# The projections' product P2 nested for pairs of rope units, and the plan's table of shifted due times left out

## Chip, cores and metric

The kernel runs on one core of one Trainium2 chip. The metric is the device time of one execution in microseconds, the median of several runs. TensorE does the matrix products, VectorE and ScalarE the elementwise work, GpSimd a little of it, and SyncE (SP) starts the transfers.

## What is computed

Two sequences of 512 tokens and width 1024 (`x_prompt`, `x_sample`) go through the same trunk of two layers.

```
x = x + diff_attention(rms_norm(x))      # layer 1: w_in 1024 x 8192 -> q, k, v, gate; w_out 2048 x 1024
x = x + bidir_retention(rms_norm(x))     # layer 2: w_in 1024 x 6144 -> q, k, v, gate; w_out 2048 x 1024
y = rms_norm(x)
```

q and k are rotated (`rotary_half`, `retention_rotate`), the gate goes through SiLU and multiplies the mixer's output ahead of `w_out`. Everything is float32. The change is in the first product of each layer, `h @ w_in`.

## The kernel before

**Three passes.** Every operand of a product is split into a high part `hi` (a rounding to fp32r, written by ScalarE, helper `hi_of`, L450) and a low part `lo = x - hi` (VectorE, `lo_of`, L453). A product is the three passes hi*hi, hi*lo, lo*hi (`PASSES`), each with its own load of the 128 x 128 stationary operand.

**Seven products.** Both sequences stand side by side: the activations B are 1024 x 1024 (width x tokens of both). They are cut into 2 x 2 blocks, B11 and B21 for the first sequence (upper and lower half of the width), B12 and B22 for the second. `make_b` builds from them the seven operands B11, B21, T1, T2, B22, T3, T4, four row tiles of 128 x 512 each, split in hi and lo and kept in slots (`B_OF`, `B_SLOT`). A `Unit` is 256 columns of `w_in`: its weights are 2 x 2 blocks of 512 x 128. It takes seven products instead of eight, in the order `SEQ`: P1 = A11*B11, P2 = A12*B21, P5, P6, P3, P7, P4. The products P5, P6, P3 and P7 have weights that are sums of blocks (`combine` in `Unit.prep`, L620, on VectorE); P1, P2 and P4 take blocks as they were loaded. A product of a "pair" unit (rope or gate) is 4 row tiles x 3 passes = 12 matmuls of 128 x 512 (L671, `Unit.product`). A "wide" unit (the values v) has 512 columns and its matmuls are 128 x 256 (L681), 48 to a product. `Unit.evac` adds the products up: ScalarE copies P1, P5 and P6's bank (L724), VectorE adds the copies to P2, P3 and P7's banks (L732).

**Units.** Layer 1 has 16 rope units (q and k of 8 heads), 8 gates and 4 wides, layer 2 has 8, 8 and 4. The first five units of a layer are gates, whose products are interleaved so that they need the operands in the order in which `make_b` has them. Behind these `mixed` puts two rope units, then a wide or a gate, and so on; layer 1 ends on six rope units and two gates. `rot_done` rotates: 4 multiplications, 2 sums and 2 splits on VectorE for each sequence of a unit, then stores. `gate_done` (L826 to L829) and `v_done` finish the others.

**Order.** `projections` walks the list of `product_order` and prepares the weights (sum, hi, lo) in a ring `ws` of `WS_BUFS` = 7 places ahead of the product that uses them. Every operation of the kernel is recorded in a `Plan` with an engine, a cost, what it reads and what it writes. `Plan.arrange` then simulates the engines and writes the order of each engine: TensorE takes products in the program's order, or passes over those that aren't ready within a window of 24; the others take what is ready by due time. `Plan.issue` repeats that for eight rounds, feeds the begins back as due times and keeps the best. On top of it lies a table `SHIFTS` of 45 entries (place in time, stretch behind it, size, share, seed). Each moves the due times of some operations near its place by random amounts, and the order is arranged again after each.

**Buffers.** `raw` (4 tiles of loaded weights), `st` (3 weight sums of 1024 columns), `c` (4 copies), `e` (8 sums), `m` (4), `os` (3 outgoing). PSUM has eight banks: pj 3, sc 2, o 2, tp 1. A rope unit in the middle of a layer uses pj for P1, P6, P7 and P4, sc for P5 and P3, o for P2 alone.

Of the kernel before, what the change touches and what calls it, by code (L numbers as in the profile page):

```python
# [16 lines left out]
P = 128  # L17
# [16 lines left out]
WS_BUFS = 7  # L34
LAG = 4
# [12 lines left out]
class Buf:  # L48
# [19 lines left out]


SHIFTS = (  # L70
# [14 lines left out]
)  # L85


class Plan:
# [167 lines left out]
    def issue(self, rounds=8):  # L256
# [29 lines left out]
def trunk_kernel(  # L286
# [14 lines left out]
    wk = ctx.enter_context(tc.tile_pool(name="wk", bufs=1))  # L301
    pj = ctx.enter_context(tc.tile_pool(name="pj", bufs=1, space=bass.MemoryType.PSUM))
# [4 lines left out]
    SIZE = dict(raw=1024, st=1024, c=512, e=512, m=512, os=1024)  # L307
# [3 lines left out]
    def view(pool, tag, i, size, shape, dt=F32):  # L311
# [3 lines left out]
        if (tag, i) not in places:  # L315
            if size <= 32 and pool in (cp, wk):
                k = next(k for k, used in enumerate(gaps) if used + size <= PAD - 32)
# [13 lines left out]
    def work(tag, shape, bufs, dt=F32, name=None):  # L331
        size = SIZE.get(tag, shape[1])
# [3 lines left out]
    gaps = [0] * (WS_BUFS - 1)  # L336
    arena = ar.tile([P, 18 * 1024 + 128], F32R, tag="arena", name="arena")
    rings, pads = [], []
    for i in range(WS_BUFS):
        rings.append(ar.tile([P, 1024 + 32], F32R, tag=f"ws{i}", name=f"ws_{i}"))  # L340
        if i < WS_BUFS - 1:
            pads.append(ar.tile([P, PAD - 32], F32, tag=f"pad{i}", name=f"pad_{i}"))

    def slot(n, shape, dt=F32R, shift=0):
# [5 lines left out]
        if at is None:  # L350
# [3 lines left out]
            return Buf(plan, f"b{n}", 1, lambda i: cp.tile(shape, dt, tag=f"b{n}", name=label))  # L354
# [13 lines left out]
    def ws_t(shape, wide=False):  # L368
# [1327 lines left out]
```

## Time and profile before

| what | value |
|---|---|
| median of 3 runs | 1790.91 us (1790.78 to 1790.96) |
| span of the profiled execution, first to last instruction | 1789.1 us |
| TensorE busy | 1780.3 us |
| VectorE busy | 1483.1 us |
| ScalarE busy | 894.0 us |
| GpSimd busy | 117.3 us |
| granted TensorE clock | 1.000 |

The profiled execution is one run with a span of 1789.1 us; the median of the timed runs is 1.8 us above that. In the profile, PE is TensorE's matmuls, PEld its weight loads (beside the matmuls), DVE VectorE, ACT ScalarE, POOL GpSimd, and SPq the transfers that SyncE issues. A group reads: line, engine, operation, names out<-in, shapes, count, then busy time, mean ns of one, and the idle time ahead of it with what ended it. In a row of windows each engine has its busy us and, in brackets, its number of instructions. A matmul's end is modelled and overlaps the next one's start, so a busy TensorE isn't yet TensorE at its pace; the distance from start to start tells that. By the stretches of the trace, the five gates and the building of B take up to some 107 us, layer 1's projections run to about 630 us, attention to about 1020, layer 2's projections to about 1490 and retention to the end.

### The profile page before, as it was taken

How to read it: one execution, taken by the hardware profiler on the slowest of the kernel's cores; microseconds unless marked ns; L12 is line 12 of the kernel's file. 1: busy time of each engine (PE TensorE's matmuls, PEld its weight loads, DVE VectorE, ACT ScalarE, POOL GpSimd, SP SyncE). 2: the span in 40 equal slices, each digit the busy share in tenths (PEclk: the TensorE clock that was granted, in tenths of full speed). 3: DMA queues.
4: the chain of work that ended last, by engine and by line, in shares of the span. 5: the costliest groups of instructions: out<-in, count | busy, mean ns of one | idle time of the engine just before them, and what ended most of it. 6: DMA issues, size and time to landing. Idle time of an engine off the chain costs nothing.

```text
span 1789.1 us, 27780 instructions
## 1 busy us (share of the span) xinstructions
PE 1780.3 (100%) x10317; PEld 1564.5 (87%) x10317; DVE 1483.1 (83%) x2401; ACT 894.0 (50%) x1866; POOL 117.3 (7%) x256
## 2 busy tenths in 40 slices
PE   9999999999999999999999999999999999999998
PEld 7889889898988888888888888898989988888887
DVE  8968788778698888888888897877887968888887
ACT  8754344343444555455445876444434455444446
POOL 1000000000000011111111100000000000111114
PEclk9999999999999999999999999999999999999999
DMA  6444554655545695455453524464646559664652
GB/s 220 138 139 142 169 164 145 192 162 153 186 118 179 205 334 205 175 188 189 170 189 124 188 75 139 149 205 165 222 135 232 166 196 395 251 228 177 235 212 95
DMA packets 162815, 328.81 MB, mean 184 GB/s; under 512 B 12772, under 2 KB 76920, under 8 KB 162680
## 3 DMA queue, kind: packets, MB, share of 16 engines
q1 hardware_dynamic: 162352, 326.71, 53.8%
q8 instruction: 81, 1.33, 0.3%
q14 instruction: 54, 0.44, 0.1%
q10 hardware_dynamic: 328, 0.34, 0.1%
HBM read 209.55 MB, written 117.44 MB: 183 GB/s over the span
## 4 chain that ended last, share of the span: by engine, by line
PE 99%; DMA 0%; ACT 0%; DVE 0%; issue 0%; POOLq 0%; SPq 0%; DVEq 0%; ACTq 0%
PE pj L671 22%; PE pj L984 20%; PE sc L671 11%; PE pj L681 10%; PE o L671 9%; PE o L1312 5%; PE sc L1251 5%; PE sc L681 5%; PE o L1521 2%; PE o L681 2%; PE sc L1477 1%; PE tp L1501 1%; PE o L1529 1%; PE pj L1292 1%; PE tp L1292 1%; PE tp L908 0%
## 5 line engine op out<-in xcount | busy, mean ns | idle before, releaser
L984 PE MATMUL pj<-ws,arena 128*128 128x512 f32 x1542 | 377.6, 392 | 0.0
L984 PEld LDWEIGHTS pj<-ws,arena 128*128 128x128 f32 x1542 | 281.8, 188 | 54.3
L671 PE MATMUL pj<-b,ws 128*128 128x512 f32 x1080 | 263.4, 390 | 0.0
L671 PEld LDWEIGHTS pj<-b,ws 128*128 128x128 f32 x1080 | 201.1, 188 | 41.0
L989 DVE SCALAR_TENSOR_TENSOR b<-pj,pad,b 128x512 f32<-128x512 f32 (+1 forms) x257 | 190.7, 745 | 24.1 <-PE pj L984 21.1
L453 DVE TENSOR_TENSOR ws<-raw,ws 128x512 fp32r<-128x512 f32 (+2 forms) x165 | 141.8, 864 | 66.6 <-ACT ws L450 56.3
L453 DVE TENSOR_TENSOR ws<-st,ws 128x512 fp32r<-128x512 f32 (+1 forms) x192 | 147.5, 774 | 55.6 <-ACT ws L450 49.5
L450 ACT CAST ws<-st 128x512 fp32r<-128x512 f32 (+1 forms) x192 | 131.9, 692 | 121.8 <-PE pj L671 42.6
L671 PE MATMUL sc<-arena,ws 128*128 128x512 f32 x768 | 185.1, 389 | 0.0
L671 PE MATMUL o<-arena,ws 128*128 128x512 f32 x744 | 178.5, 391 | 0.0
L450 ACT CAST ws<-raw 128x512 fp32r<-128x512 f32 (+2 forms) x165 | 126.1, 769 | 88.6 <-PE o L671 48.3
L671 PEld LDWEIGHTS sc<-arena,ws 128*128 128x128 f32 x768 | 144.0, 188 | 29.7
L671 PEld LDWEIGHTS o<-arena,ws 128*128 128x128 f32 x744 | 138.4, 188 | 28.5 <-DVE arena L513 0.2
L671 PE MATMUL pj<-arena,ws 128*128 128x512 f32 x636 | 156.0, 390 | 0.0
L671 PEld LDWEIGHTS pj<-arena,ws 128*128 128x128 f32 x636 | 118.6, 188 | 24.3
L1269 ACT ACTIVATE b<-sc,pad 128x512 f32<-128x512 f32 x128 | 87.6, 692 | 74.1 <-DVE pad L1259 74.0
L724 ACT COPY c<-pj 128x512 f32<-128x512 f32 x104 | 60.8, 586 | 117.8 <-PE pj L671 67.7
L681 PE MATMUL pj<-ws,b 128*128 128x256 f32 x960 | 116.9, 275 | 0.0
L681 PEld LDWEIGHTS pj<-ws,b 128*128 128x128 f32 x960 | 113.3, 188 | 0.6
L1251 PE MATMUL sc<-arena 128*128 128x512 f32 x384 | 101.3, 397 | 0.0
L1312 PEld LDWEIGHTS o<-arena 128*128 128x128 f32 x768 | 93.0, 188 | 2.5
L1312 PE MATMUL o<-arena 128*128 128x256 f32 x768 | 93.6, 277 | 0.0
(229 smaller groups left out, 2827.4 us busy)
## 6 DMA issues: line engine op xcount, KB each, us to landing
qk<-os SPq DMA_DIRECT2D x192, 256.0 KB, 3.5
arena<-qk SPq DMA_DIRECT2D x96, 512.0 KB, 6.6
v<-os SPq DMA_DIRECT2D x64, 512.0 KB, 5.2
arena<-v SPq DMA_DIRECT2D x64, 512.0 KB, 4.1
raw<-in_da_w_in_dram SPq DMA_DIRECT2D x63, 512.0 KB, 5.1
raw<-in_ret_w_in_dram SPq DMA_DIRECT2D x48, 512.0 KB, 4.9
os<-g SPq DMA_DIRECT2D x32, 512.0 KB, 7.9
g<-e SPq DMA_DIRECT2D x48, 256.0 KB, 4.7
```

The lines of the kernel that those rows point to most:

```text
L450: act(n, lambda: nc.scalar.copy(dst(), src()), r, w)
L453: dve(n, lambda: nc.vector.tensor_tensor(dst(), src(), hi().bitcast(F32), op=ALU.subtract), r, w)
L671: nc.tensor.matmul(ps.t, a[u][0]()[:, k, :], bt[k][:, v, :], start=(opens and k == 0 and i == 0), stop=(k == 3 and i == 2), skip_group_che ...
L681: nc.tensor.matmul(ps[:, (t % 2) * 256:(t % 2) * 256 + 256], bt[k][:, v, t * P:(t + 1) * P], a[u][0]()[:, k, :], start=(opens and t % 2 == ...
L724: act(S, lambda c=c, ps=ps: nc.scalar.copy(c.t, ps.t), [ps], [c])
L984: nc.tensor.matmul(ps[:, here], o[a][:, e, t * P:(t + 1) * P], u[b][:, e, here], start=(m == 0), stop=(m == 5))
L989: axpy(n, lambda half=half, here=here, ps=ps: nc.vector.scalar_tensor_tensor(half, ps[:, here], rr[:, t % 2:t % 2 + 1], half, op0=ALU.mult ...
L1251: nc.tensor.matmul(s.t, q[:, a, t * P:(t + 1) * P], k[:, b, :], start=(n == 0), stop=(n == 2))
L1269: act(840, lambda j=j, s=s, m=m: nc.scalar.activation(p[:, j, :], s.t, AF.Exp, bias=m.t, accum_out=sm[:, 2 * j + n:2 * j + n + 1]), [s, m] ...
L1292: nc.tensor.transpose(tp[:, j * P:(j + 1) * P], p[:, 0, j * P:(j + 1) * P], ident.t)
L1312: nc.tensor.matmul(o[:, e * 256:(e + 1) * 256], v[b][:, j, e * P:(e + 1) * P], aT[a][:, j, :], start=(n == 0), stop=(n % 12 == 11), skip_g ...
L1521: nc.tensor.matmul(o[:, e * 256:(e + 1) * 256], v_[v][:, 2 * c + j, e * P:(e + 1) * P], a_[:, u, j * 256:(j + 1) * 256], start=(e == 0 and ...
```

## The change

P2 = A12*B21 of two rope units u and v that stand side by side becomes one nested product of a new class `Duo`. Its weights are 2 x 2 blocks of 256 x 128: the upper and lower halves of u's A12 and of v's A12. B21 is cut into 2 x 2 blocks of 256 x 256. The same seven-product scheme is used within: seven inner products of 2 row tiles x 3 passes = 6 matmuls of 128 x 256.

- `Duo.prep`: the four weight sums run on GpSimd (`pool`), the splits as before on ScalarE and VectorE, in halves of 256 where blocks come straight from the loaded weights.
- `Duo.product`: the inner products share the two banks o (`yu`, `yv`). Halves that later products add to are kept by a ScalarE copy and a GpSimd addition of the unit's copy of P1 (`kept`); the last ones are added on VectorE (`added`).
- `product_order`: for such a pair P1 of u, the last unit's P4, P1 of v, then D0 to D3 between u's P5, P6, P3 and P7, then v's P5, u's P4 and the rest of v. Units that stand alone and the early gates keep their order.
- `make_b`: the four block operands t1 to t4 of B21 are made once a layer by `inner_blocks`, eight subtractions of 256 columns on GpSimd and four splits, in one working tile one after the other; t3's split comes at the very end. T4's subtraction, which overwrites B21's copy, comes behind the blocks' reads.
- Room: three new places of 1024 columns (28, 29 and 30), the seventh place of the ring holds t2, so that the projections prepare in `PROJ_WS` = 6 places (the out projections keep 7). `st` is 4 tiles of 512 columns, and a wide unit's sums and their splits are made in two halves. `e` has 6 tiles. The retention's decay tables move from `st` to places 28 and 29; two temporaries of `make_b` move from `e` to place 30.
- `SHIFTS` and the loop over it in `Plan.issue` are removed.

The core of the diff (left out: the table's lines, the layout of pads, the halves of wide sums and the counts passed to `step`):

```diff
+        def inner_blocks(h):
+
+            def quarter(k, n):
+                return (lambda: h[k][0]()[:, n * 256:n * 256 + 256]), h[k][1]
+
+            def block(name, pairs, tile):
+                x = tile
+                for j, (a, b) in enumerate(pairs):
+                    pool(256, lambda j=j, a=a, b=b: nc.gpsimd.tensor_tensor(x[:, j], a[0](), b[0](), op=ALU.subtract),
+                         [a[1], b[1]], [(x, j)])
+                if name != "t3":
+                    stored(name, x)
+
+            def stored(name, x):
+                o = slot(dict(t1=28, t4=29, t3=30)[name], [P, 2, 2, 256]) if name != "t2" else spare_ring(32)
+                hi_of(S, lambda: o[:, 0], lambda: x.t, [x], [(o, 0)])
+                lo_of(S, lambda: o[:, 1], lambda: x.t, lambda: o[:, 0], [x, (o, 0)], [(o, 1)])
+                Bop["B21", name] = o
+
+            def part(x):
+                return [((lambda j=j: x[:, j]), (x, j)) for j in range(2)]
+            x = work("e", [P, 2, 256], E_BUFS, name="tt")
+            block("t1", [(quarter(j, 1), quarter(j, 0)) for j in range(2)], x)
+            block("t2", list(zip([quarter(2 + j, 1) for j in range(2)], part(x))), x)
+            block("t4", list(zip([quarter(2 + j, 0) for j in range(2)], part(x))), x)
+            block("t3", [(quarter(2 + j, 1), quarter(j, 1)) for j in range(2)], x)
+            return lambda: stored("t3", x)
...
-        out, span, begin, starts = best
-        shift = {}
-        for at, back, by, part, seed in SHIFTS:
-            rng = random.Random(seed)
-            for n, e in out:
-                if e != "PE" and at - back <= begin[n] <= at + 6.0 and rng.random() < part:
-                    shift[n] = shift.get(n, 0.0) + rng.gauss(0.0, by)
-            out, begin, span = self.arrange(starts, shift)
-        self.best = best = (out, span, begin)
+        self.best = best
...
+    class Duo:
+
+        n_ws, wide, early = 1, False, None
+        STEPS = ("D0", "D1", "D2", "D3")
+
+        def __init__(self, u, v):
+            self.u, self.v, self.w = u, v, {}
+
+        def raw(self, u, k):
+
+            def fn():
+                t = u.take(0, 1)[0]()
+                if len(t.shape) == 3:
+                    t = t.rearrange("p k (j i) -> p k j i", j=2)
+                return t[:, 2 * k:2 * k + 2]
+            return fn
+
+        def prep(self, op):
+            u, v = self.u, self.v
+            xu, xv = u.take(0, 1)[1], v.take(0, 1)[1]
+            a11, a12, a21, a22 = (self.raw(x, k) for x in (u, v) for k in range(2))
+            four = lambda t: t.rearrange("p (k j i) -> p k j i", k=2, j=2)
+
+            def put(x, at, a, b, fn, r):
+                out = lambda: four(x[:, at * 256:at * 256 + 256])
+                pool(256, lambda: nc.gpsimd.tensor_tensor(out(), a(), b(), op=fn), r, [(x, at)])
+                return out
+            w = self.w[op] = ws_t([P, 1024], 4 if op in ("D1", "D3") else 36)
+            if op == "D0":
+                for k, src in enumerate((a11, a12)):
+                    hi, lo = (lambda k=k, u=u: four(w[:, u * 512 + k * 256:u * 512 + k * 256 + 256]) for u in range(2))
+                    hi_of(256, hi, src, [xu], [(w, (0, k))])
+                    lo_of(256, lo, src, hi, [xu, (w, (0, k))], [(w, (1, k))])
+                return
+            if op == "D3":
+                hi, lo = (lambda u=u: four(w[:, u * 512 + 256:u * 512 + 512]) for u in range(2))
+                hi_of(256, hi, a22, [xv], [(w, (0, 1))])
+                lo_of(256, lo, a22, hi, [xv, (w, (0, 1))], [(w, (1, 1))])
+                hi, lo = (lambda u=u: w[:, u * 512:u * 512 + 256] for u in range(2))
+                s3 = lambda: self.late[:, 256:512]
+                hi_of(256, hi, s3, [(self.late, 1)], [(w, (0, 0))])
+                lo_of(256, lo, s3, hi, [(self.late, 1), (w, (0, 0))], [(w, (1, 0))])
+                return
+            x = st_t([P, S])
+            if op == "D1":
+                s1 = put(x, 0, a21, a22, ALU.add, [xv])
+                self.s2 = put(x, 1, s1, a11, ALU.subtract, [xu, (x, 0)]), (x, 1)
+            else:
+                self.late = x
+                put(x, 0, a12, self.s2[0], ALU.subtract, [xu, self.s2[1]])
+                put(x, 1, a11, a21, ALU.subtract, [xu, xv])
+                hi, lo = (lambda u=u: w[:, u * 512:u * 512 + 256] for u in range(2))
+                s4 = lambda: x[:, 0:256]
+                hi_of(256, hi, s4, [(x, 0)], [(w, (0, 0))])
+                lo_of(256, lo, s4, hi, [(x, 0), (w, (0, 0))], [(w, (1, 0))])
+                return
+            hi, lo = (lambda u=u: w[:, u * 512:u * 512 + 512] for u in range(2))
+            hi_of(S, hi, lambda: x.t, [x], [(w, (0, None))])
+            lo_of(S, lo, lambda: x.t, hi, [x, (w, (0, None))], [(w, (1, None))])
+
+        def inner(self, op, n, ps, c0, block, start):
+
+            w = self.w[op]
+            plain = block in ("b11", "b21", "b22")
+            bt = [Bop["B21", k] for k in range(4)] if plain else [Bop["B21", block]]
+
+            def of(v, j):
+                if plain:
+                    c = 256 * (block == "b22")
+                    return bt[2 * (block in ("b21", "b22")) + j][:, v, c:c + 256]
+                return bt[0][:, v, j, :]
+
+            def fn():
+                for j in range(2):
+                    for i, (a, b) in enumerate(PASSES):
+                        lo = a * 512 + n * 256 + j * P
+                        nc.tensor.matmul(ps[:, c0:c0 + 256], w[:, lo:lo + P], of(b, j),
+                                         start=(start and j == 0 and i == 0), stop=(j == 1 and i == 2),
+                                         skip_group_check=True)
+            pe(0.681, fn, [w, *bt], [ps])
+
+        def product(self, op):
+            u, v = self.u, self.v
+
+            def kept(e, c, ps, lo, c1):
+                act(256, lambda: nc.scalar.copy(e[:, c:c + 256], ps[:, lo:lo + 256]), [ps], [(e, c)])
+                pool(256, lambda: nc.gpsimd.tensor_tensor(
+                    e[:, c:c + 256], e[:, c:c + 256], c1[:, c:c + 256], op=ALU.add), [(e, c), c1], [(e, c)])
+
+            def added(n, e, c, ps, lo, x):
+                dve(n, lambda: nc.vector.tensor_tensor(e[:, c:c + n], ps[:, lo:lo + n], x[:, c:c + n], op=ALU.add),
+                    [ps, x if n == S else (x, c)], [e if n == S else (e, c)])
+            if op == "D0":
+                self.yv, self.yu = bank("o"), bank("o")
+                self.eu, self.ev = e_t(), e_t()
+                self.inner(op, 0, self.yv, 0, "b11", True)
+                kept(self.eu, 0, self.yv, 0, u.s["c1"][0])
+                self.inner(op, 1, self.yu, 0, "b21", True)
+            elif op == "D1":
+                self.inner(op, 0, self.yu, 256, "t1", False)
+                kept(self.ev, 256, self.yu, 256, v.s["c1"][0])
+                self.inner(op, 1, self.yv, 0, "t2", False)
+                kept(self.eu, 256, self.yv, 0, u.s["c1"][0])
+            elif op == "D2":
+                self.inner(op, 0, self.yu, 256, "b22", False)
+                added(S, self.eu, 0, self.yu, 0, self.eu)
+                u.done(0, 0, [self.eu], u.s, False)
+            else:
+                self.inner(op, 0, self.yv, 0, "t3", False)
+                added(256, self.ev, 256, self.yv, 0, self.ev)
+                self.inner(op, 1, self.yv, 0, "t4", False)
+                added(256, self.ev, 0, self.yv, 0, v.s["c1"][0])
+                v.done(0, 0, [self.ev], v.s, False)
+
...
+        left = list(units[n:-1])
+        duos[0] = 0
+        while left:
+            u = left.pop(0)
+            v = left[0] if left else None
+            if v and u.kind == v.kind == "pair" and u.done.__qualname__ == v.done.__qualname__:
+                left.pop(0)
+                d = Duo(u, v)
+                duos[0] += 1
+                out += [(u, "P1"), tail, (v, "P1"), (d, "D0"), (u, "P5"), (d, "D1"), (u, "P6"), (d, "D2"), (u, "P3"),
+                        (d, "D3"), (u, "P7"), (v, "P5"), (u, "P4"), (v, "P6"), (v, "P3"), (v, "P7")]
+                tail = (v, "P4")
+                continue
```

More of the change, by code (lines that the diff above doesn't have):

```diff
@@ L316, in view @@
             if size <= 32 and pool in (cp, wk):
-                k = next(k for k, used in enumerate(gaps) if used + size <= PAD - 32)
+                k = next(k for k, used in enumerate(gaps) if used + size <= (1024 + PAD - RING if k < WS_BUFS - 1 else 56))
                 places[tag, i] = pads[k][:, gaps[k]:gaps[k] + size]
@@ L376, in make, with spare_ring @@
             return t.rearrange("p (a b c) -> p a b c", a=shape[1], b=shape[2])
-        return Buf(plan, "ws", WS_BUFS, make)
+        b = Buf(plan, f"ws{bufs}", bufs, make)
+        b.also = Buf(plan, f"ring{b.nth % bufs}", 1, None)
+        return b
+    def spare_ring(lo):
+        b = Buf(plan, "spare", 1, lambda i: rings[PROJ_WS][:, lo:lo + 1024].rearrange(
+            "p (a b c) -> p a b c", a=2, b=2))
+        b.also = Buf(plan, f"ring{PROJ_WS}", 1, None)
+        return b
     def raw_t(shape):
@@ L555, in make_b @@
                 yield
-        t = [whole(e_t("h")), whole(e_t("h")), half(two[2], 0), half(two[2], 1)]
+        both = slot(30, [P, 2, S], F32)
+        t = [half(both, 0), half(both, 1), half(two[2], 0), half(two[2], 1)]
         for k in range(4):
@@ L621, in combine, with halves_of @@
                 return out
+            def halves_of(a):
+                if isinstance(a, list):
+                    return a
+                return [((lambda k=k: a[0]()[:, 2 * k:2 * k + 2]), a[1]) for k in range(2)]
             if op == "P1":
@@ L875, in projections @@
                 v, p = order[ready]
-                if sum(w.n_ws for w, _ in order[n:ready]) + v.n_ws > WS_BUFS:
+                if sum(w.n_ws for w, _ in order[n:ready]) + v.n_ws > PROJ_WS:
                     break
```

63 lines of the change are left out of this document (43 added, 20 removed), and 14 rows, old and new, of the table SHIFTS.

## The prediction

> **What bounds the kernel now.** I read the page first, then the waits of TensorE, then stretches of 25 us, then counts around the tile that holds the split weights.
>
> ```profile
> span 1789.1 us, 27780 instructions
> PE 1780.3 (100%) x10317; PEld 1564.5 (87%) x10317; DVE 1483.1 (83%) x2401; ACT 894.0 (50%) x1866; POOL 117.3 (7%) x256
> PE 99%; DMA 0%; ACT 0%; DVE 0%; issue 0%; POOLq 0%; SPq 0%; DVEq 0%; ACTq 0%
> ```
>
> ```profile
> PE sc L1115 <- DVE pad L463: 1.2, 1, 1.2
> PE sc L1174 <- ACT b L434: 0.6, 1, 0.6
> PE pj L474 <- DMA m<-in_ret_subln_g_dram: 0.4, 1, 0.4
> ```
>
> The chain that ends last is TensorE at 99%, and its listed waits come to 2.2 us, all before the first product. No other engine, transfer or wait stands on the path. So TensorE work that goes is gain one for one, and each new hole in TensorE is loss one for one.
>
> Columns of the next two: TensorE, weight loads, VectorE, ScalarE, GpSimd (the second has no GpSimd).
>
> ```profile
> 50.00:75.00 25.00, 25.00 (x112) 20.71 (x111) 25.00 (x43) 17.62 (x31) 0.00 (x0) 1.00 0.33 111
> 300.00:325.00 25.00, 25.00 (x211) 24.50 (x210) 15.93 (x24) 11.15 (x19) 0.00 (x0) 1.00 0.54 177
> 469.00:583.00 114.00, 114.00 (x537) 95.67 (x536) 96.90 (x158) 45.33 (x80) 0.00 (x0) 1.00 0.53 164
> 1028.00:1092.00 64.00, 64.00 (x292) 53.15 (x291) 61.44 (x101) 45.67 (x80) 0.00 (x0) 1.00 0.27 91
> ```
>
> ```profile
> 0.00:60.00 60.00, 45.07 (x197) 35.21 (x198) 10.81 (x17) 10.89 (x19) 1.00 0.54 190
> 0.00:80.00 80.00, 65.07 (x285) 51.78 (x286) 16.18 (x25) 14.51 (x26) 1.00 0.50 175
> 0.00:100.00 100.00, 85.07 (x373) 68.36 (x374) 24.08 (x37) 21.32 (x37) 1.00 0.50 172
> 0.00:140.00 140.00, 125.07 (x550) 101.47 (x551) 34.23 (x51) 30.43 (x51) 1.00 0.48 161
> ```
>
> The second fence is filtered to tile ws, so VectorE's count is weight splits done and TensorE's is matmuls that used them. The first product has 24 matmuls and two splits, every other 12 and one. At 60 us, (197-24)/12+1 = 15.4 products have begun and 16 are split; at 80 us 22.8 and 24; at 100 us 30.1 and 36; at 140 us 44.8 and 50. **The lead is about one product up to 80 us, where VectorE is busy 25.00 of 25, and five to six from 100 us on.** In the first place any extra VectorE work stops TensorE. In the second it eats into some 11 us of lead (five products less the time of a preparation).
>
> **The change, part by part.** Pitches first, from starts of neighbouring rows of the timeline:
>
> ```profile
> 61.79 5.60 PE L671 MATMUL pj<-b,ws 128*128 128x512 f32 x24
> 67.23 2.88 PE L671 MATMUL o<-arena,ws 128*128 128x512 f32 x12
> ...
> 307.35 5.60 PE L681 MATMUL sc<-ws,arena 128*128 128x256 f32 x48
> 312.79 5.60 PE L681 MATMUL pj<-ws,b 128*128 128x256 f32 x48
> ```
>
> 5.44 us for 24 of 512 columns is 0.2267 each; 5.44 for 48 of 256 is 0.1133 each, exactly half.
>
> *Products.* Two units' P2 are now 24 matmuls of 512, 5.44 us. Nested they are seven inner products of 2 row tiles x 3 passes = 42 of 256, 42 x 0.1133 = 4.76. A pair saves 0.68. Behind the five early units, layer 1 has 8 rope pairs side by side and layer 2 has 4; no two gates stand together there. 12 x 0.68 = **-8.2 us**. The rows of 256 already include a new weight load each: weight loads are busy 24.50 of 25 there and TensorE keeps its pitch.
>
> By the Trainium skill, "Perfetto Trace Analysis", Identifying the Most-Contended Engine, the share of weight loads and not that of matmuls tells TensorE's headroom. That speaks against trading wide matmuls for more narrow ones; by the rows above the pitch holds, and the sum would be the same.
>
> *VectorE and GpSimd in the projections.*
>
> ```profile
> 521.41 0.68 DVE L620 TENSOR_TENSOR st<-st,raw 128x512 f32<-128x512 f32 x1
> 522.02 0.68 DVE L453 TENSOR_TENSOR os<-m,os 128x512 fp32r<-128x512 f32 x1
> ...
> L901 DVE TENSOR_TENSOR m<-m 128x256 f32<-128x256 f32 x64 | 26.6, 416 | 0.0
> L453 DVE TENSOR_TENSOR ws<-st,ws 128x512 fp32r<-128x512 f32 x160 | 108.5, 685 | 49.8 <-ACT ws L450 49.5
> L450 ACT CAST ws<-st 128x512 fp32r<-128x512 f32 x160 | 98.1, 620 | 76.0 <-PE pj L671 35.8 <-PE sc L671 12.2 <-issue 10.0
> L1568 POOL TENSOR_TENSOR e<-b,cos 128x512 f32<-128x512 f32 x7 | 9.4, 1340 | 0.0
> ```
>
> A VectorE operation of 512 follows the one before by 0.60 (0.68 with overlap); one of 256, 0.42 with the same 0.08 of overlap, by about 0.33. A rope unit has 30 of 512: 7 splits, 4 weight sums, 3 product sums, 16 in the rotation and its stores. That is 18.1 us against 7 x 2.72 = 19.0 of TensorE. Nested, a pair's P2 has splits of 1 x 512 and 5 x 256 instead of 2 x 512, and sums of 512 + 2 x 256 instead of 2 x 512: +1.1 us. So a pair goes from 36.1 beside 38.1 to 37.2 beside 37.4. VectorE then only just keeps pace, but with five products of lead at the outset nothing is late; a ring of six in place of seven takes one off. Single pairs lie between wide units and gates, where VectorE is busy 15.93 of 25. Cost **0**; without that lead it would be the 0.4 us by which wait and work could miss, per pair, 5 at most. The seven GpSimd operations of a pair (four sums, three additions) are half of 1.34 each, 0.67, or 4.7 us of 37.4 on an engine with nothing else there; ScalarE (45.33 of 114) hides its added copies. The wide units' combinations in two halves add pitch of under 0.5 us a unit to a VectorE with 9 us spare. No DMA is added; SP's and GpSimd's queues issue the same transfers. Six e buffers for eight I also cost at 0: a pair takes six and the oldest is free a pair later.
>
> *Blocks of B21.* Each layer's start gets 8 GpSimd subtractions, 4 splits on ScalarE and 4 on VectorE. The T4 subtractions on VectorE now come behind them, as they overwrite what the blocks read. Queued behind T4 are its splits, then the P4 products of the first units. Three of the four splits lie ahead of T4 and all in the stretch with a lead of one: 3 x 0.60 = **+1.8 us** in layer 1. The bounds are 0 (the gates' deferred work moves further back) and 2.4. In layer 2 VectorE has 64 - 61.44 = 2.6 us spare: 0, at most 2.4.
>
> *The table.* The list of 45 shifts of due times goes. The plan's order is then its best of eight unshifted rounds. No row of before shows that order, so I bound it by what small holes still stand:
>
> ```profile
> 38.33 0.60 PE L1147 MATMUL o<-ident,b 128*128 128x128 f32 x4
> 38.68 2.99 PE L671 MATMUL sc<-arena,ws 128*128 128x512 f32 x12
> 41.51 0.60 PE L1147 MATMUL o<-ident,b 128*128 128x128 f32 x4
> 42.12 3.04 PE L671 MATMUL o<-arena,ws 128*128 128x512 f32 x12
> ```
>
> A product takes 2.83 here against 2.72, 0.1 over; four transposes take 0.61 against 0.35, 0.26 over. If each entry removes one hole of 0.1, the table is worth 4.5 us; the ends are 0 and 45 x 0.26 = 11.7. I take **+4.5**, since the first kind of hole is the commoner in the rows.
>
> **Sum.** 1789.1 - 8.2 + 1.8 + 4.5 = 1787.2 for the span; the median of the runs lies 1.8 above the profiled span, so **1789.0**. Against 1790.91 that is 0.1% less. About 0.2%, or 3.6 us, is what a measurement of this kernel can tell from no change.
>
> **Rivals.**
>
> *The saving stays (faster).* For it: TensorE is unbroken over 500 us with VectorE up to 97 of 114 busy, so the plan has slack nearly everywhere and eight rounds may find it unaided. Then the table is worth 1 to 2 and the blocks up to 1: 1790.9 - 8.2 + 2.3 = 1785.0; with nothing lost 1782.7.
>
> *GpSimd takes VectorE's time at the layers' starts (slower).* For it:
>
> ```profile
> 1760.26 0.68 DVE L453 TENSOR_TENSOR arena<-c,arena 128x512 fp32r<-128x512 f32 x1
> 1760.51 1.59 POOL L1568 TENSOR_TENSOR e<-b,cos 128x512 f32<-128x512 f32 x1
> ...
> 1766.44 1.30 POOL L1568 TENSOR_TENSOR e<-b,cos 128x512 f32<-128x512 f32 x1
> ```
>
> The GpSimd product that began inside a VectorE split with both inputs in SBUF took 0.29 longer than the one that didn't, as if it waited for the split's end. The reverse would hold VectorE for up to 0.6 per GpSimd operation of 256.
>
> By the Trainium skill, "SBUF — State Buffer", Who interferes with whom, a VectorE instruction with two SBUF inputs contends with a GpSimd one that reads SBUF, and the loser waits for the whole instruction. The 0.29 us agrees in one direction; no row of before shows VectorE held.
>
> Against it:
>
> ```profile
> 1750.21 0.75 DVE L989 SCALAR_TENSOR_TENSOR b<-pj,pad,b 128x512 f32<-128x512 f32 x1
> 1750.39 0.70 POOL L916 TENSOR_TENSOR pad<-pad,pad 128x2 f32<-128x2 f32 x1
> 1750.87 0.68 DVE L453 TENSOR_TENSOR arena<-c,arena 128x512 fp32r<-128x512 f32 x1
> ```
>
> A two-input split started on time inside a (tiny) GpSimd operation. Price: layer 1's start 8 x 0.6 = 4.8; layer 2's 4.8 + 2.4 of splits - 2.6 spare = 4.6; the stretch from 469 to 583 us loses 21 x 0.6 = 12.6, about what its lead covers, 0 to 2. 1789.0 + 9.4 = 1798.4. It decides from 0.34 us per operation of the sixteen (5.5 us together, past 1794.5).
>
> *The narrow products don't run at half the pitch, or the plan without the table is far worse.* With 5.44 / 42 = 0.1295 per matmul nothing is saved: 1797.2. The rows at 307 us speak against that. The table at its upper end of 11.7 gives 1796.2.
>
> **How the numbers follow.** The forecast of 1789.0, from 1787.4 to 1794.5 by its own bounds, has 0.37. The saving that stays has 0.33. GpSimd's hold has 0.21, the last rival 0.09. So faster by over 0.2% is 0.33, within it 0.37, slower 0.30. The range is 1784 to 1800: it leaves out some 0.07 below, where next to nothing is lost, and 0.1 above, where hold and table add up.
>
> **What would show it.** Right: 12 x 18 = 216 more matmuls, nested ones 0.68 us per six, no TensorE wait between 100 and 600 us, new holes of 2 to 6 us between 25 and 90 us. GpSimd's hold: VectorE operations with two SBUF inputs longer than 0.68, or starting late, beside GpSimd operations. Wrong throughout: waits of TensorE on bank o or on splits inside the pairs, which would mean that the lead of five products was not there.

## The result and the profile after

| | before | after |
|---|---|---|
| median of the runs | 1790.9 us | 1809.78 us (4 runs, 1808.69 to 1810.08) |
| ratio, 95% interval | | 1.0104 [1.009, 1.0119] |
| span of the profiled execution | 1789.1 us | 1807.8 us |

The change costs 18.9 us. The forecast was 1789.0 and the range ended at 1800. No clear change and a faster kernel had 0.70 together, a slower one 0.30.

From the page of the changed kernel: the span, the busy times, and the chain that ended last.

```profile
span 1807.8 us, 28903 instructions
PE 1781.4 (99%) x10533; PEld 1570.2 (87%) x10533; DVE 1538.0 (85%) x2535; ACT 924.6 (51%) x1988; POOL 245.8 (14%) x356
...
PE 85%; DVE 7%; DMA 2%; POOL 2%; issue 1%; ACT 1%; SPq 1%; POOLq 0%; DVEq 0%; ACTq 0%
```

The 216 more matmuls are there (10533 against 10317), and TensorE is busy for about as long as before, in a span that is 18.7 longer. So most of the loss stands beside the matmuls and not in them: the chain, TensorE at 99% before, now runs through VectorE for 7% and GpSimd for 2%.

Waits of TensorE in the changed kernel (us in total, times, longest):

```profile
PE pj L712 <- DVE os L442: 7.4, 6, 1.7
PE o L870 <- DVE e L884: 2.9, 2, 1.4
PE o L712 <- DVE b L502: 1.8, 1, 1.8
PE o L712 <- DVE arena L502: 1.2, 1, 1.2
```

Before, the listed waits came to 2.2 us, none in the projections. The first row is new, six times in the middle of the projections: product P1 waits for VectorE's evacuation of a pj bank (L442, lo_of). The second, twice, is a nested product that waits for L884, the sum that empties bank o.

Busy times by stretches, of before and then of after (TensorE, weight loads, VectorE, ScalarE, GpSimd, each with its count):

```profile
0.00:100.00 100.00, 97.88 (x460) 80.89 (x461) 91.28 (x171) 77.98 (x142) 5.92 (x12) 1.00 0.50 172
100.00:600.00 500.00, 500.00 (x2878) 440.12 (x2877) 401.30 (x614) 208.99 (x346) 0.00 (x0) 1.00 0.51 158
...
1000.00:1100.00 100.00, 100.00 (x476) 83.70 (x475) 90.30 (x145) 76.97 (x152) 4.88 (x8) 1.00 0.44 149
```

```profile
0.00:100.00 100.00, 94.56 (x441) 77.18 (x442) 91.24 (x169) 76.80 (x139) 15.56 (x20) 1.00 0.51 174
100.00:600.00 500.00, 492.04 (x2990) 438.02 (x2989) 424.49 (x674) 223.28 (x412) 81.56 (x56) 1.00 0.50 155
...
1000.00:1100.00 100.00, 97.54 (x486) 81.86 (x486) 89.27 (x142) 76.34 (x164) 17.94 (x23) 1.00 0.39 131
```

The stretch from 100 to 600 us, unbroken before and with the long lead, loses 8.0 us of TensorE. There VectorE is busy 23 us longer and GpSimd, once idle, has 56 operations in 81.56 us: 1.46 each, where I had 0.67.

The busy time leaves out parts of a hole, since it counts a matmul's whole drain. So I also took each matmul's start to the next one's start, less the usual pitch of its size, and summed all that is above 0.06 us, by stage:

```
us of holes          before  after  e2    e3    e4    e5    e6    e7    e9    e10
12 to 100 us           1.6    5.8   5.9   4.1   2.3   4.7   4.5   5.7   2.9   4.1
100 to 600             0.1    9.7   3.7   3.1   0.1   0.1   0.1   3.3   0.1   0.1
600 to 660             0.7    1.8   1.2   2.0   2.1   2.0   2.1   2.0   0.7   1.6
1000 to 1130           0.5    3.9   3.8   3.8   4.4   6.0   3.7   3.8   2.9   3.7
1130 to 1500           1.5    4.2   1.4   1.4   1.4   1.4   1.5   2.9   1.5   1.5
```

(e2 and the rest are the experiments below; in the stages left out the holes move by 0.2 us or less.) All stages of the span together: products -8.2, holes +21.2, the rest of the pitch +4.7 (2.7 of it at the nested matmuls), the end behind the last matmul +0.9, in all +18.6 of 18.7.

**A hole behind a wide unit.** From the timeline of the changed kernel around 330 us (start, duration, engine):

```profile
326.14 1.23 DVE L442 TENSOR_TENSOR ws<-st,ws 128x512 fp32r<-128x512 f32 x1
...
326.89 1.08 POOL L818 TENSOR_TENSOR st<-st,raw 128x256 f32<-128x256 f32 x1
327.29 1.23 DVE L648 TENSOR_TENSOR st<-st,raw 128x512 f32<-128x512 f32 x1
...
328.05 1.07 POOL L818 TENSOR_TENSOR st<-raw,st 128x256 f32<-128x256 f32 x1
328.44 1.23 DVE L442 TENSOR_TENSOR os<-e,os 128x512 fp32r<-128x512 f32 x1
...
329.08 1.18 POOL L818 TENSOR_TENSOR st<-raw,raw 128x256 f32<-128x256 f32 x1
329.59 1.23 DVE L648 TENSOR_TENSOR st<-raw,st 128x512 f32<-128x512 f32 x1
...
330.74 0.68 DVE L442 TENSOR_TENSOR ws<-st,ws 128x512 fp32r<-128x512 f32 x1
331.24 0.58 ACT L439 CAST os<-pj 128x512 fp32r<-128x512 f32 x1
331.52 0.69 DVE L648 TENSOR_TENSOR st<-raw 128x512 f32<-128x512 f32 x1
332.13 0.68 DVE L442 TENSOR_TENSOR os<-pj,os 128x512 fp32r<-128x512 f32 x1
...
332.87 3.02 PE L712 MATMUL pj<-arena,ws 128*128 128x512 f32 x12 [1.71 <-DVE os L442]
```

The four weight sums on GpSimd (L818; the first began at 325.80) stand beside four VectorE operations with both inputs in SBUF. Each of those takes 1.23 in place of 0.68; behind the last GpSimd operation the next takes 0.68 again. VectorE so reaches the evacuation `os<-pj` at 332.13 some 2.2 us late (4 x 0.55). TensorE's next product is P1 of the pair's second unit: the order `(u,P1), tail, (v,P1)` opens a third pj bank right behind the wide unit's P4, and one of the banks of that product is the one that is late. It stops for 1.71 us, for the bank and not for weights: no listed wait of TensorE is on a split in tile ws. The same place in e10 below, where every engine's order is the same but the new GpSimd operations read nothing, has the evacuation done at 327.98, and TensorE goes on without a stop as the wide product ends:

```profile
327.30 0.68 DVE L442 TENSOR_TENSOR os<-pj,os 128x512 fp32r<-128x512 f32 x1
...
328.18 2.91 PE L712 MATMUL pj<-arena,ws 128*128 128x512 f32 x12
```

**A hole inside a pair**, from the timeline around 540 us:

```profile
535.95 7.33 POOL L880 TENSOR_TENSOR e<-e,c 128x256 f32<-128x256 f32 x1 [3.85 <-ACT e L879]
...
541.40 0.68 DVE L442 TENSOR_TENSOR ws<-st,ws 128x512 fp32r<-128x512 f32 x1
542.00 0.68 DVE L442 TENSOR_TENSOR os<-m,os 128x512 fp32r<-128x512 f32 x1
...
544.00 0.69 DVE L884 TENSOR_TENSOR e<-o,e 128x512 f32<-128x512 f32 x1 [1.32 <-POOL e L880]
...
545.21 0.41 DVE L884 TENSOR_TENSOR e<-o,e 128x256 f32<-128x256 f32 x1
...
545.68 0.98 PE L870 MATMUL o<-b,ws 128*128 128x256 f32 x6 [1.42 <-DVE e L884]
```

Here GpSimd is the one held: a single addition of 256 columns takes 7.33 us, beside twelve VectorE operations with both inputs in SBUF that run back to back and take no longer than alone (0.68 for 512 columns). It ends 0.6 us after the last of these; the addition behind it, with VectorE standing still, takes 0.74 and ends at 543.97. VectorE's next operation in its order is a sum that needs these halves, so it stops 1.32 us for GpSimd, and D3's second inner product 1.42 us for the bank.

### The profile page after: what moved, and what is told of

It is laid out like the page before. It is cut to its first block, busy times and chain, and to the rows that moved or that the text cites. A ratio compares the mean times of both kernels' runs of the same rounds, so it can differ in the third digit from the quotient of the medians.

```text
span 1807.8 us, 28903 instructions
## 1 busy us (share of the span) xinstructions
PE 1781.4 (99%) x10533; PEld 1570.2 (87%) x10533; DVE 1538.0 (85%) x2535; ACT 924.6 (51%) x1988; POOL 245.8 (14%) x356
## 4 chain that ended last, share of the span: by engine, by line
PE 85%; DVE 7%; DMA 2%; POOL 2%; issue 1%; ACT 1%; SPq 1%; POOLq 0%; DVEq 0%; ACTq 0%
PE pj L1159 19%; PE pj L712 17%; PE sc L712 10%; PE pj L722 8%; PE o L1487 5%; PE sc L1426 5%; PE o L712 4%; PE sc L722 4%; PE o L870 3%; PE o L1696 2%; PE o L722 2%; DVE ws L442 2%; PE sc L1652 1%; PE tp L1676 1%; PE o L1704 1%
## 5 line engine op out<-in xcount | busy, mean ns | idle before, releaser
L439 ACT CAST ws<-st 128x512 fp32r<-128x512 f32 (+1 forms) x260 | 153.3, 601 | 167.1 <-PE o L870 47.5
L442 DVE TENSOR_TENSOR ws<-st,ws 128x512 fp32r<-128x512 f32 (+1 forms) x260 | 176.9, 691 | 41.9 <-ACT ws L439 41.4
L442 DVE TENSOR_TENSOR ws<-raw,ws 128x512 fp32r<-128x512 f32 (+2 forms) x177 | 143.1, 816 | 31.3 <-ACT ws L439 26.9
L722 PEld LDWEIGHTS pj<-ws,b 128*128 128x128 f32 x960 | 113.3, 188 | 0.6
L712 PE MATMUL o<-arena,ws 128*128 128x512 f32 x456 | 108.5, 390 | 3.0 <-DVE b L502 1.8
L712 PEld LDWEIGHTS o<-arena,ws 128*128 128x128 f32 x456 | 85.1, 188 | 21.0 <-ACT ws L439 2.0
L439 ACT CAST os<-e 128x512 fp32r<-128x512 f32 x96 | 59.1, 621 | 79.6 <-DVE e L773 29.6
```

Of the source, the lines that this page charges most:

```text
L439: act(n, lambda: nc.scalar.copy(dst(), src()), r, w)
L442: dve(n, lambda: nc.vector.tensor_tensor(dst(), src(), hi().bitcast(F32), op=ALU.subtract), r, w)
L712: nc.tensor.matmul(ps.t, a[u][0]()[:, k, :], bt[k][:, v, :], start=(opens and k == 0 and i == 0), stop=(k == 3 and i == 2), skip_group_che ...
L722: nc.tensor.matmul(ps[:, (t % 2) * 256:(t % 2) * 256 + 256], bt[k][:, v, t * P:(t + 1) * P], a[u][0]()[:, k, :], start=(opens and t % 2 == ...
```

## The experiments

The theories, as the expectations name them: **P**, the port: GpSimd's SBUF reads and VectorE's two-SBUF-input operations hold each other up, and banks come free late. **B**, the bank order: the order of the units' products behind a wide unit leaves no time to free a bank. **T**: the table of shifts that is gone. **R**: the rest, smaller buffers, the ring of six and the missing table. **L**: GpSimd's operations are only slow, come late in a chain, and VectorE waits for them. One more, without a letter, is the load: VectorE has simply more to do than its lead covers. Each time is compared with the kernel before on the same chip (medians 1790.86 to 1790.95).

**e1: the kernel before without its table.**

```diff
-SHIFTS = ( ... 45 entries ... )
+SHIFTS = ()
```

> The kernel before with the table of 45 shifts emptied and nothing else changed. Theory T (the loss is the plan's order without the table): at least 10 us over before, 1801 or more, with new TensorE holes in all three layers' projections. Theory P (GpSimd and VectorE hold each other up wherever the new GpSimd work meets VectorE operations with two SBUF inputs) and theory B (behind a wide unit v's P1 has to wait for one of that unit's pj banks): the table is worth little, 1791 to 1795. The prediction on record had 4.5 us for it: 1795.4.

1793.29 us, ratio 1.0013 [1.0003, 1.0022]. The table is worth 2.4 us; my 4.5 was too much, and T, which wanted 1801 or more, is out.

**e2: the changed kernel with another order of two products.**

```diff
-out += [(u, "P1"), tail, (v, "P1"), (d, "D0"), (u, "P5"), (d, "D1"), ...
+out += [(u, "P1"), tail, (d, "D0"), (u, "P5"), (v, "P1"), (d, "D1"), ...
```

> The changed kernel with v's P1 put behind D0 and u's P5 in the order of products, so that a wide unit's last product has 4 us more before a third pj bank is opened. Theory B: the six holes of TensorE behind wide units (0.8 to 2.0 us each, 8.5 together) go, 1801 to 1803. Theory P: the banks are free late because VectorE's evacuation is held up by GpSimd's weight sums; the holes shrink by some and turn up at the next wait, 1805 to 1809. Theory T: no change, 1809 to 1811.

1799.56 us, 1.0048 [1.0033, 1.0063]: 10.2 less than the change, with no operation taken out, and lower than any theory expected. The waits on `os` behind wide units are gone. One GpSimd addition (L880) still takes as long, but VectorE's combinations (L648) are at 745 ns, where the changed kernel has 822 and e10 below 686:

```profile
L880 POOL TENSOR_TENSOR e<-e,c 128x256 f32<-128x256 f32 x36 | 50.0, 1401 | 241.7 <-ACT e L879 233.0 <-DVE st L648 8.6
...
L648 DVE TENSOR_TENSOR st<-st,raw 128x512 f32<-128x512 f32 x40 | 29.7, 745 | 0.6
```

VectorE is busy for 1526.8 us, 11.2 less than in the changed kernel, with the same 2535 operations. So the edit does two things: it gives the late bank more time, and the order that the planner makes of it has fewer VectorE operations stretched. Where GpSimd has none of this work, from e3 to e6, the same edit is worth 2.6 us.

**e3: the changed kernel with all 100 new GpSimd operations on VectorE.** The three places are the block subtractions (L534), the weight sums (L818) and the additions of copies (L880).

```diff
-pool(256, lambda: nc.gpsimd.tensor_tensor(out(), a(), b(), op=fn), r, [(x, at)])
+dve(256, lambda: nc.vector.tensor_tensor(out(), a(), b(), op=fn), r, [(x, at)])
```

> The changed kernel with all of its new GpSimd work (8 block subtractions a layer, 4 weight sums and 3 additions a pair, 100 operations of 256) put on VectorE. Theory P: no VectorE operation of 512 takes over 0.70 us any more; VectorE gets 100 x 0.33 = 33 us more work and is still quicker, 1795 to 1801. Theory B: the waits for the pj bank stay and VectorE is fuller, 1809 to 1815. Theory T: no gain, 1809 or more.

1797.97 us, 1.0040 [1.0025, 1.0055]: 11.8 less, with 100 more operations of about 0.42 us on VectorE. Even so its busy time, 1536.7 us, isn't above the 1538.0 of the changed kernel: the hold had cost VectorE as much as these operations do. If the load alone decided, this had to be slower. Three waits on `os` behind wide units stay, 1.9 us in all.

**e4: the changed kernel without nested products and blocks**; the buffers, the halves and the missing table stay.

```diff
-if v and u.kind == v.kind == "pair" and ...
+if False and v and u.kind == v.kind == "pair" and ...
-        more = inner_blocks(h21)
-        more()
```

> The changed kernel with every unit's P2 a plain product again and without the blocks of B21; six ring places, the smaller e and st buffers, the halves of the wide sums and the missing table stay. It computes the same. Theories P and B: the loss sits in the nested products' own work, so this comes near before plus the table, 1792 to 1796. Theory R (the rest: the smaller buffers, the ring of six and the missing table): 1803 or more.

1795.79 us, 1.0030 [1.0018, 1.0041]: R, which wanted 1803 or more, is out. It is 2.5 above e1, which I had costed at 0. Its holes stand from 600 to 660 us (2.1) and near 1020 us (4.4).

**e5: e4 with the blocks made and not used.**

```diff
+        more = inner_blocks(h21)
+        more()
```

> The kernel of e4_no_duo with the four blocks of B21 made and used by nobody: 8 GpSimd subtractions, 4 ScalarE and 4 VectorE splits a layer. It computes the same. Theory P: in the start of layer 1, where the lead is one product, the 1.8 us of splits ahead of T4 and GpSimd's hold on VectorE come back as TensorE holes, e4 + 2 to 4: 1798 to 1800; layer 2's start has room and gives 0 to 1. Theory that the start's loss is the order alone: as e4, 1795.8.

1801.77 us, 1.0060 [1.0045, 1.0075]: the blocks cost 6.0 by the medians, more than expected (4.3 between the two profiled spans, as the profiled run of e4 is 1.4 above its median). From 25 to 100 us, e4 and then e5:

```profile
25.00:100.00 75.00, 75.00 (x347) 61.99 (x346) 71.48 (x121) 55.93 (x97) 1.86 (x3) 1.00 0.38 122
```

```profile
25.00:100.00 75.00, 73.20 (x336) 59.92 (x335) 73.87 (x121) 55.90 (x98) 10.08 (x11) 1.00 0.36 114
```

In the same 75 us VectorE does as many operations (121), and they take 2.4 us longer, with eight more operations on GpSimd: five of VectorE's 512-column operations, each beside a block subtraction, take 0.91 to 1.23. Another five do so at layer 2's start; e4 has none. TensorE starts 11 matmuls less.

**e6: e2 and e3 together.**

> e2 and e3 together: v's P1 behind D0 and u's P5, and all of the new GpSimd work on VectorE. If both act on the same holes (VectorE held up makes a bank late, the order gives the bank time), little adds up: no hole over 0.5 us between 100 and 600 us, e3 less 3 to 5: 1793 to 1795. If they were separate losses, their gains add: 1809.8 - 10.2 - 11.8 = 1787.8. Theory B alone: as e2.

1795.34 us, 1.0026 [1.0015, 1.0036]: 14.4 less than the change. The parts alone gave 10.2 and 11.8, so they overlap by 7.6: both work on the same holes. No wait of TensorE is left between 100 and 600 us. Its longest waits:

```profile
PE o L712 <- DVE b L502: 1.8, 1, 1.8
PE o L712 <- DVE arena L502: 1.2, 1, 1.2
PE sc L1290 <- DVE pad L452: 1.2, 1, 1.2
```

**e7: only the weight sums on VectorE** (one of e3's three edits, at L818).

> The changed kernel with only the pairs' weight sums (48 operations of 256) on VectorE; the additions behind ScalarE's copies (36) and the blocks (16) stay on GpSimd. Theory P has two halves: the weight sums meet the splits and make the bank behind a wide unit late (8.5 us, goes with this edit), and the additions of a dense stretch wait on VectorE and make the last inner products late (3 us between 530 and 590 us, stays). So 1800 to 1803. If the additions were the main loss it would stay at 1807 or more.

1800.61 us, 1.0052 [1.0037, 1.0067]: the 48 weight sums alone bring 9.2 of e3's 11.8. The other 52 operations bring 2.6 on top of that.

**e8: e6 with the nested products' weights at the other offset of their buffer**, to see whether the address sets the nested pitch.

```diff
-w = self.w[op] = ws_t([P, 1024], 4 if op in ("D1", "D3") else 36)
+w = self.w[op] = ws_t([P, 1024], 36 if op in ("D1", "D3") else 4)
```

> e6 with the columns at which the nested products' weights begin in their ring place exchanged (36 for D1 and D3, 4 for D0 and D2, where it was 4 and 36). Only the address of the stationary operand against that of the moving one changes. If the address sets the pitch of the nested matmuls (118.6 ns in the changed kernel against 113.5 in a wide unit), the 504 of them move together by some ns each, 1 to 4 us in all, in either direction; if not, the same as e6 within 0.5 us.

1793.9 us, 1.0016 [1.0007, 1.0026], 1.4 below e6, but not for the reason tried: the mean nested pitch went from 118.6 to 118.3 ns, 0.2 us over 504 matmuls. Of the rest 0.4 lies at layer 1's start and about 0.7 behind the last matmul. So which product has which of the two offsets doesn't set the pitch; other addresses weren't tried.

**e9: e8 with a table of its own** (26 shifts, searched for this plan) and the planner's cost of an inner product at 0.711.

```diff
+SHIFTS = ( ... 26 entries ... )
-pe(0.681, fn, [w, *bt], [ps])
+pe(0.711, fn, [w, *bt], [ps])
```

> e8 with a table of 26 shifts of its own (found with the plan's simulation, as the old one's form is) and the plan's cost of a nested inner product at 0.711 us instead of 0.681. Theory: what still stands in e8 above the kernel before is order, about 2.5 us in layer 1's start, 1.4 us ahead of attention and 3.2 us in layer 2's start; the table takes away most of it: 1786 to 1789, under both kernels. Rival: these holes come from the buffers (ring of six, six e) and from VectorE's extra work, and no order removes them: 1791 to 1794.

1790.06 us, 0.9996 [0.9987, 1.0005]: 19.7 less than the change, equal to the kernel before and not better: both the 1786 to 1789 expected and the rival's 1791 to 1794 were missed.

**e10: the changed kernel with its 100 new GpSimd operations replaced by fills of the same 256 columns**, in the same place of every engine's order. It leaves out the block subtractions, the weight sums and the additions of copies. In the two traces TensorE, VectorE and ScalarE have the same operations in the same order.

```diff
-pool(256, lambda: nc.gpsimd.tensor_tensor(out(), a(), b(), op=fn), r, [(x, at)])
+pool(256, lambda: nc.gpsimd.memset(out(), 0.0), r, [(x, at)])
```

> The changed kernel with each of its 100 new GpSimd operations replaced by a memset of the same 256 columns: the block subtractions, the weight sums and the additions of the copies are left out, everything else and each engine's order stay. A memset writes SBUF and reads nothing. Theory P (GpSimd's reads and VectorE's second input exclude each other): no VectorE operation of 512 over 0.70 us beside one of these, and about e3's gain, 1795 to 1799. Rival L (GpSimd's operations only come late in a chain, since they are slow, and VectorE is held by waiting on them): operations of 512 beside them stay at 1.0 to 1.2 us, 1803 or more.

1794.06 us, 1.0018 [1.0009, 1.0027]: 15.7 less. The groups of the changed kernel, and then those of e10 (count, busy us and mean ns):

```profile
L442 DVE TENSOR_TENSOR ws<-st,ws 128x512 fp32r<-128x512 f32 x236 | 167.5, 719 | 41.9 <-ACT ws L439 41.4 <-PE pj L722 0.2
...
L880 POOL TENSOR_TENSOR e<-e,c 128x256 f32<-128x256 f32 x36 | 50.1, 1406 | 123.6 <-ACT e L879 118.5 <-DVE st L648 5.1
...
L648 DVE TENSOR_TENSOR st<-st,raw 128x512 f32<-128x512 f32 x40 | 32.8, 822 | 0.5
...
L818 POOL TENSOR_TENSOR st<-raw,st 128x256 f32<-128x256 f32 x12 | 17.2, 1431 | 0.9
```

```profile
L648 DVE TENSOR_TENSOR st<-st,raw 128x512 f32<-128x512 f32 x40 | 27.4, 686 | 0.5
...
L818 POOL MEMSET st<- 128x256 f32 x48 | 13.5, 312 | 457.5 <-DVE ws L442 451.5 <-ACT ws L439 6.0
...
L880 POOL MEMSET e<- 128x256 f32 x36 | 11.2, 312 | 322.6 <-ACT e L879 298.0 <-DMA g<-m 23.8
```

GpSimd still has as many operations, but they read nothing, and VectorE's combinations are back at 686 ns from 822; under L they had to stay stretched. VectorE's busy time falls from 1538.0 to 1505.8 us, and holes between 100 and 600 us go from 9.7 to 0.1, with the change's own bank order. So without the reads there is nothing here for a better order to mend. (The fills are also shorter, 0.31 us, so this run by itself doesn't tell the reads from the length of GpSimd's operations. That VectorE's operations with one input in PSUM aren't stretched beside the same GpSimd operations, as shown further on, speaks for the reads.)

**e11: e4 with one ring of seven split weights** in place of six, shared with the out projections.

```diff
-PROJ_WS = 6
+PROJ_WS = 7
```

> e4 (no nested products, no blocks, no table) with seven ring places for the projections again, in one ring with the out projections as before; the smaller e and st and the halves of the wide sums stay. If the ring of six makes the holes where a stage hands over to the next (about 3.5 us around 1020 to 1050 us in e4), this comes to 1793, the time of the kernel before without its table. If the e and st buffers make them, it stays at 1795 to 1796.

1794.98 us, 1.0023 [1.0014, 1.0032], 0.8 below e4. The holes from 1000 to 1060 us shrink from 4.4 to 1.0, while those from 12 to 60 us grow from 2.1 to 4.2. Which buffer costs e4 its 2.5 us isn't settled: each such edit also gives the planner another order.

**e12: e9 with the out projections on the ring of six, the kept halves added by one VectorE operation straight from PSUM**, a higher planned cost of GpSimd's power at the end of attention (800 in place of 200), and a table of its own (13 shifts).

```diff
-hi, lo = ws_t([P, 2, S], 0, WS_BUFS), ws_t([P, 2, S], 0, WS_BUFS)
+hi, lo = ws_t([P, 2, S]), ws_t([P, 2, S])
-act(256, lambda: nc.scalar.copy(e[:, c:c + 256], ps[:, lo:lo + 256]), [ps], [(e, c)])
...
-    e[:, c:c + 256], e[:, c:c + 256], c1[:, c:c + 256], op=ALU.add), [(e, c), c1], [(e, c)])
+    e[:, c:c + 256], ps[:, lo:lo + 256], c1[:, c:c + 256], op=ALU.add), [ps, c1], [(e, c)])
...
-r = row_norm(g, t)
+r = row_norm(g, t, 800)
```

> e9 with three edits and a table of its own: the out projections take the same ring of six in turn as the projections (so no place is held across two rings), a kept half of a nested bank is one VectorE addition from PSUM instead of a ScalarE copy and an addition, and the plan counts 2.1 us instead of 0.6 for GpSimd's power of a row's norm at the end of attention (it took 2.73 us in e9 while VectorE ran splits with two SBUF inputs). Theory: what e9 has over the kernel before around 1025 us, 2.5 us of TensorE holes, is GpSimd's late power and the two rings; most of it goes: 1787 to 1789, faster than before by 0.1 to 0.2%. Rival: the holes there are VectorE's own load, or the waits turn up elsewhere, 1790 to 1792.

1790.72 us, 1.0000 [0.9991, 1.0009]. No gain over e9; 2.4 us of holes stay from 1000 to 1130 us, against 2.9 in e9.

The steps from before to after, by the medians:

| | us | step |
|---|---|---|
| before | 1790.9 | |
| e1, no table | 1793.3 | +2.4 |
| e4, smaller buffers and halves | 1795.8 | +2.5 |
| e5, blocks made | 1801.8 | +6.0 |
| after, nested products | 1809.8 | +8.0 |

## Why the prediction was wrong, by its steps

**Products, -8.2: the count was right, the pitch not quite.** The 504 nested matmuls follow one another by 118.6 ns in place of 113.3. From the timeline of the changed kernel:

```profile
533.01 0.87 PE L870 MATMUL o<-b,ws 128*128 128x256 f32 x6
...
533.72 0.87 PE L870 MATMUL o<-ws,ws 128*128 128x256 f32 x6
...
534.43 1.55 PE L712 MATMUL pj<-b,ws 128*128 128x512 f32 x6
```

Six take 0.71 us, where the text wanted 0.68: +2.7 us in all. The rival with narrow products at 0.1295 was wrong by more.

**The projections' work on VectorE and GpSimd, 0: this is the step that failed.** From e5 to the changed kernel the nested products cost 8.0 net of their gain: +8.2 for the work saved, so some 16.2 us of loss. Of these 2.7 are the nested pitch and 11.2 stand in holes by the table above, 9.6 of them between 100 and 600 us; the rest is a slightly longer pitch of other matmuls and the end. Three things in the step were wrong. First, "0.67, or 4.7 us of 37.4 on an engine with nothing else there" took half the mean of seven GpSimd operations at the kernel's end. Beside VectorE in the projections an addition takes 1.41 on average and a weight sum 1.07 to 1.43, and VectorE is held as well, which the step didn't have at all. Second, "with five products of lead at the outset nothing is late" counted split weights. TensorE never waited for them here; it waited for PSUM banks, whose evacuation stands in the same VectorE queue, and the lead doesn't cover a bank. Third, I looked inside the pairs, and six of the eight holes stand at their beginning, where `(v,P1)` needs a bank from the wide unit before. The text's own mark for this, "waits of TensorE on bank o or on splits inside the pairs", is met by two of the eight.

**GpSimd's hold: the right mechanism, in the wrong place.** I saw from a row of 0.29 us that the two engines meet in SBUF, gave it 0.21, and put it at the layers' starts. There it holds too, but less than priced: the rival's 9.4 for both starts came on top of the 1.8 of the blocks' splits, and e5 has 6.0 for both together. The stretch where I set 0 to 2 us, "about what its lead covers", cost most. The runs that decide are e10 (same order, no reads: -15.7) and e3 (off GpSimd: -11.8). By the rule of the Trainium skill that the prediction cites ("SBUF — State Buffer", Who interferes with whom), a VectorE operation with two SBUF inputs contends with a GpSimd one that reads SBUF, and one with at most one SBUF input, outside VectorE's two-port modes, doesn't. The trace agrees: beside GpSimd operations with two inputs in SBUF, as `ws<-st,ws` or `st<-st,raw`, go up to 1.23, while `e<-o,c`, with one input in PSUM, has 0.68 both alone and beside GpSimd (rows below). The second half of the rule, that the loser waits for one whole instruction, is less than what the row at 535.95 us shows: one GpSimd addition in 7.33 us, over twelve operations of VectorE. One of each kind beside GpSimd, from the timeline of the changed kernel:

```profile
112.08 1.23 DVE L648 TENSOR_TENSOR st<-st,raw 128x512 f32<-128x512 f32 x1
112.84 1.07 POOL L818 TENSOR_TENSOR st<-raw,st 128x256 f32<-128x256 f32 x1
113.23 0.68 DVE L773 TENSOR_TENSOR e<-o,c 128x512 f32<-128x512 f32 x1
```

**Blocks, +1.8: mis-sized.** 6.0; the holes grow by 2.4 at layer 1's start and 1.6 at layer 2's, where I had 0. The ten stretched VectorE operations of e5 come to 5.0 us over their usual times, so the hold, which the forecast's sum left out, is there; how the 6.0 divides between hold and splits wasn't tested.

**The table, +4.5: mis-sized.** 2.4.

**Buffers, six e and a ring of six, 0: mis-sized.** 2.5 together with the halves (e4). That it comes from a buffer and not from the order that the planner makes of it was not shown.

**What the measured terms give.** The table, the buffers, the pitch and the blocks as measured already give 1790.9 + 2.4 + 2.5 + 6.0 - 8.2 + 2.7 = 1796.3, slower by 0.3%, before any hole inside the projections. By e10 most of the loss is one thing: 15.7 of the 18.9 us go when the new GpSimd operations fill in place of reading. But the 3.2 that stay are still no gain, and at best (e9) the saving of 8.2 pays for the pitch and for what blocks and buffers cost, and nothing is left.

## What to carry to other kernels

Before you move work to an idle GpSimd, count its SBUF reads beside VectorE operations that have both inputs in SBUF: here 0.42 us of VectorE work became on average about 1.3 us of GpSimd and 0.32 us more of VectorE each (the busy times of the changed kernel and of e10), and moving it back was 11.8 us faster. A lead counted in one resource (split weights) says nothing of another (PSUM banks): for each product, look at which bank it opens, and which operation, in which queue, sets that bank free. When two edits mend the same holes, as e2 and e3 do, their gains don't add; run them together before you credit either.

## What the runs showed of the hardware

**GpSimd can be held for much longer than one operation.** Not only the additions: a power of 128x1, whose mean before was 0.61 us, took 2.73 in e9. From its timeline:

```profile
1022.60 0.68 DVE L461 TENSOR_TENSOR arena<-m,arena 128x512 fp32r<-128x512 f32 x1
1022.75 2.73 POOL L1217 TENSOR_TENSOR pad<-pad,pad 128x1 f32<-128x1 f32 x1 [3.51 <-ACT pad L1210]
...
1023.20 0.68 DVE L461 TENSOR_TENSOR ws<-raw,ws 128x512 fp32r<-128x512 f32 x1
1023.80 1.28 DVE L461 TENSOR_TENSOR arena<-m,arena 128x512 fp32r<-128x512 f32 x2
...
1025.51 1.15 ACT L442 ACTIVATE b<-b,pad 128x1024 f32<-128x1024 f32 x1 [1.88 <-POOL pad L1217]
...
1026.71 0.33 PE L1341 MATMUL sc<-ident,b 128*128 128x128 f32 x1 [1.39 <-ACT b L442]
```

It ends 0.40 us after VectorE's run of splits (1025.08), and through ScalarE it makes a hole of 1.39 us in TensorE. No edit touched this operation; the eight powers at this place of the kernel before took 0.54 to 0.85. Spans on GpSimd are rough, but ScalarE's wait for it isn't.

**It goes both ways, and which way isn't explained.** At 326 us VectorE's operations were stretched to 1.23 and GpSimd's took 1.1; at 536 us VectorE kept 0.68 and GpSimd's one addition took 7.33. Both have operations with two SBUF inputs at a like density. What decides stays open.

**Nested matmuls of 256 columns run at 118.6 ns, those of the wide units at 113.3**, with a weight load to each in both. Exchanging the weights' two offsets changed 0.3 ns of it (e8). What else differs (operands in two tiles, alternating halves of a bank) wasn't tried; the cause stays open.
